# Five Strassen pairs a round in place of three, and row tiles that reach y by an accumulating DMA

## The chip, the cores and the metric

The kernel runs on one core of one Trainium2 chip. The metric is the device time of one execution in microseconds (us), as a median of runs. One more execution is recorded by the hardware profiler; its rows are quoted below.

## The reference

One encoder layer on 256 tokens of width 2048, in float32: a gated feed-forward block (FFN), a mixing block (attention beside a Fourier branch), and a second FFN. The change touches the two FFNs alone. Each computes

```python
def _swiglu(x, w_gate, w_up, w_down):
    return (jax.nn.silu(x @ w_gate) * (x @ w_up)) @ w_down

def _macaron_ffn(x, pre_g, w_gate, w_up, w_down, post_g):
    return x + MACARON_WEIGHT * _rms_norm(_swiglu(_rms_norm(x, pre_g), w_gate, w_up, w_down), post_g)
```

with x of [256, 2048], w_gate and w_up of [2048, 5632] and w_down of [5632, 2048].

## The kernel before, in words

**Products.** Every float32 operand is split in two parts of a shorter type, hi (ScalarE writes it by a copy, line 102) and lo (VectorE subtracts hi from the operand, line 103). One product of a 128x128 activation tile with a 128x512 weight tile is three matmuls on TensorE (`mm3`, lines 107 to 109): hi by hi, hi by lo, lo by hi.

**Weights.** They stream from HBM in pieces of 128x1024 (512 KB, two tiles). `raw_piece` loads a piece by a DMA on SyncE's queue into one of five raw buffers (RAW_BUFS), and `ring` splits it into one of six ring buffers (RING), each with a hi and a lo. A raw buffer comes free when its last reader on ScalarE or VectorE is done, a ring buffer when TensorE's last matmul on it is done.

**Rounds.** An FFN has 11 blocks of 512 hidden columns. Blocks 0 and 1 go through `col_block`. For blocks 2 to 10 the loop at the end of `ffn` runs rounds: `row_line` multiplies the block before the last by its rows of w_down (4 column blocks `cb`, 8 pieces, 12 matmuls each) and adds the result to y, an SBUF buffer; then `swiglu` computes gate and up of the round's own block, with K = 2048 as 16 tiles. A tenth `row_line` follows. That makes nine rounds in each FFN, 18 in all. In the middle of a row_line, ahead of its last column block, `ahead` transposes the h of the block before (8 small matmuls on TensorE, two splits).

**Strassen.** Two K tiles (a pair) times two token tiles by gate and up is a 2x2 by 2x2 block product, eight products if plain. For the pairs in BY_SEVEN `seven` takes Strassen-Winograd's seven: VectorE forms sums of weight tiles (`minus`, line 538: three into a buffer t13, one in place in a raw buffer), four splits follow (three of 128x1024, one of 128x512). In the text F, S, T and Q are these four pieces in their order (6, 6, 6 and 3 matmuls) with the number of their pair; g and u are the two pieces of a plain pair (12 matmuls each), r1 to r8 those of a row_line. Before, BY_SEVEN names groups of four K tiles: the first pair of groups 0, 1 and 2 is done by seven. The activation side is prepared once for each FFN by `Forms.chunk`, four K tiles a call, all four calls during the `col_block`s of block 1.

**Order.** The loop stands under a manual schedule: VectorE, ScalarE and TensorE run their instructions in the order of the program. `Line.feed` makes the preparation of a piece (`ready`: loads, minus, splits) run six pieces ahead of the matmuls (`use`); the work behind a piece's matmuls (`then`: adds, silu, copies into y) stands after `use`, ahead of the next `ready`.

**Into y.** `row_line.out` copies the first round's tiles to y on ScalarE (line 621); in all later rounds VectorE adds them, from PSUM, into y (line 623), eight tiles of 128x512 a round.

Of the kernel before, what the change touches and what calls it, by code (L numbers as in the profile page):

```python
# [18 lines left out]
P = 128  # L19
# [37 lines left out]
def encoder_layer(  # L57
# [371 lines left out]
    class Forms:  # L429
# [3 lines left out]
        def __init__(self, u, rs):  # L433
            self.u, self.rs, self.seven, self.plain = u, rs, {}, {}
            self.rooms = {}

        def room(self, n):

            for i, used in self.rooms.items():
                if used[0] + n <= D:  # L440
                    break
            else:
                i = len(self.rooms)
                used = self.rooms[i] = [0] + [big(f"f{c}{i}", F32R) for c in "hl"]
            used[0] += n
            return [a[:, used[0] - n:used[0]] for a in used[1:]]

# [10 lines left out]
        def chunk(self, kg):  # L458
            ks = slice(kg * CK, (kg + 1) * CK)
            a = chunk.tile([P, CK, S], F32, tag="ch_hi", name="un")  # L460
            for t in range(NT):
                V.tensor_tensor(out=a[:, :, t * P:(t + 1) * P], in0=self.u[t][0][:, ks, :].bitcast(F32),
                                in1=self.u[t][1][:, ks, :].bitcast(F32), op=ALU.add)
            V.tensor_tensor(out=a[:], in0=a[:], in1=self.r[:].unsqueeze(1).to_broadcast([P, CK, S]), op=ALU.mult)
            n = 0
            if kg in BY_SEVEN:
                n = 2
                f = chunk.tile([P, 7, P], F32, tag="ch_lo", name="sf")
                a11, a12, a21, a22 = a[:, 0, 0:P], a[:, 1, 0:P], a[:, 0, P:S], a[:, 1, P:S]
                A.activation(f[:, 0:2, :], a[:, 0:2, 0:P], AF.Copy)  # L470
                A.activation(f[:, 2, :], a22, AF.Copy, scale=-1.0)
                V.tensor_tensor(out=f[:, 3, :], in0=a21, in1=a22, op=ALU.add)
                V.tensor_tensor(out=f[:, 4, :], in0=f[:, 3, :], in1=a11, op=ALU.subtract)
                V.tensor_tensor(out=f[:, 5, :], in0=a11, in1=a21, op=ALU.subtract)
                V.tensor_tensor(out=f[:, 6, :], in0=a12, in1=f[:, 4, :], op=ALU.subtract)
                hi, lo = (x.rearrange("p (a b) -> p a b", b=P) for x in self.room(7 * P))
                split(hi, lo, f[:])
                self.seven[kg] = [(hi[:, i, :], lo[:, i, :]) for i in range(7)]
            hi, lo = (x.rearrange("p (a b) -> p a b", b=S) for x in self.room((CK - n) * S))
            split(hi, lo, a[:, n:, :])  # L480
            for k in range(n, CK):
                self.plain[kg * CK + k] = [(hi[:, k - n, t * P:(t + 1) * P], lo[:, k - n, t * P:(t + 1) * P]) for t in range(NT)]

# [34 lines left out]
    def swiglu(line, forms, w, hs):  # L518
# [38 lines left out]

        def seven(kg, end):
            a11, a12, na22, s1, s2, s3, s4 = forms.seven[kg]
            h = {}  # L560

            def first():
                ra, rb = raw_piece(w[kg], 0), raw_piece(w[kg], 1)
                t = chunk.tile([P, WP, NB], F32, tag=("ch_hi", "ch_lo")[kg % 2], name="t13")
                h.update(ra=ra, rb=rb, t=t)
# [11 lines left out]
            def two(n, a, m, b, last):  # L577
                def use(ws):
# [50 lines left out]
    def ffn(u, rs, wg, wu, wgu, wd, yname, tail, gate0, w_next=None, early=()):  # L629
# [30 lines left out]
        with tc.manual_schedule(engines={mybir.EngineType.DVE, mybir.EngineType.Activation, mybir.EngineType.PE}):  # L660
            for f in range(PLAIN, nblk + 1):
# [568 lines left out]
def _pairs(g, u):  # L1230


    cut = lambda w: w[:, PLAIN * NB:].reshape(KD // CK, CK, P, -1, NB).transpose(3, 0, 2, 1, 4)
    g, u = cut(g), cut(u)
    seven = [g[..., 0, :], u[..., 0, :], u[..., 1, :], g[..., 1, :], g[..., 2, :], g[..., 3, :], u[..., 2, :], u[..., 3, :]]
    plain = [g[..., 0, :], g[..., 1, :], u[..., 0, :], u[..., 1, :], g[..., 2, :], g[..., 3, :], u[..., 2, :], u[..., 3, :]]
    out = np.stack(plain, 3)
    for kg in BY_SEVEN:
        out[:, kg] = np.stack([a[:, kg] for a in seven], 2)
    return np.ascontiguousarray(out).reshape(*out.shape[:3], 2 * CW)  # L1240

# [47 lines left out]
```

## Time and profile before

| | |
|---|---|
| median of 3 runs | 2040.54 us (2039.6 to 2041.2) |
| profiled execution, own time | 2041.46 us |
| its span on the engines | 2039.7 us |
| TensorE busy | 2018.3 us, 99% |
| VectorE busy | 1651.9 us, 81% |
| ScalarE busy | 1112.2 us, 55% |
| GpSimd busy | 50.9 us, 2% |
| granted TensorE clock | 0.999 of full speed |

The span is what the profiler saw from first to last instruction; the time of the execution is 1.8 us longer. PE is TensorE's matmul side and PEld its weight loads, DVE is VectorE, ACT is ScalarE, POOL is GpSimd, SP is SyncE (SPq and POOLq: their queues).

### The profile page before, as it was taken

What the parts mean: (1) busy time and instruction counts of PE and PEld (TensorE: products, weight loads), DVE (VectorE), ACT (ScalarE), POOL (GpSimd) and SP (SyncE); (2) the same over time, 40 slices, a digit from 0 to 9 for tenths busy, and PEclk for the clock granted to TensorE, in tenths of its full rate; (3) what the DMA queues carried; (4) which work ended last, traced back from release to release, by engine and by line L of the source; (5) the groups of instructions that cost most, each with busy time, mean ns of one, the idle gap of its engine ahead of it and who ended that gap; (6) DMA issues with size and microseconds to landing.
All of it is one profiled execution on the core that took longest, in us unless ns stands there. A gap on an engine that the chain in (4) does not pass through costs nothing.

```text
span 2039.7 us, 25718 instructions
## 1 busy us (share of the span) xinstructions
PE 2018.3 (99%) x9308; PEld 1673.0 (82%) x9308; DVE 1651.9 (81%) x2216; ACT 1112.2 (55%) x1490; POOL 50.9 (2%) x46
## 2 busy tenths in 40 slices
PE   9999999999999999999999999999999999999998
PEld 7888888888888878888888888788888888888886
DVE  6878888888888788887877895877788888888876
ACT  7554555544555556556666554555554555544553
POOL 0000000000000110100000000200000000000002
PEclk9999999999999999999999999999999999999999
DMA  8675566556666696964555557566665566656663
GB/s 315 212 271 178 190 218 205 193 175 201 209 207 190 208 294 194 271 187 138 192 190 188 183 179 276 186 207 225 220 203 173 192 218 204 196 174 198 211 209 106
DMA packets 118736, 417.43 MB, mean 205 GB/s; under 512 B 12968, under 2 KB 19120, under 8 KB 116432
## 3 DMA queue, kind: packets, MB, share of 16 engines
q1 hardware_dynamic: 114256, 411.66, 61.1%
q0 software_dynamic: 4352, 4.13, 1.4%
q8 instruction: 73, 1.20, 0.2%
q14 instruction: 55, 0.45, 0.1%
HBM read 409.44 MB, written 6.29 MB: 204 GB/s over the span
## 4 chain that ended last, share of the span: by engine, by line
PE 93%; DVE 4%; DMA 1%; ACT 1%; issue 0%; SPq 0%; DVEq 0%; ACTq 0%
PE pc L108 19%; PE pc L109 19%; PE pc L107 19%; PE pr L109 10%; PE pr L107 10%; PE pr L108 10%; PE pt L177 1%; DVE wlo L103 1%; DMA raw<-in_w_fo 1%; DVE h L390 0%; PE pe L107 0%; PE pe L109 0%; PE pe L108 0%; PE pt L976 0%; PE pf L109 0%
## 5 line engine op out<-in xcount | busy, mean ns | idle before, releaser
L102 ACT ACTIVATE whi<-raw 128x1024 fp32r<-128x1024 f32 (+1 forms) x711 | 749.0, 1059 | 618.8 <-PE pc L109 268.2
L103 DVE TENSOR_TENSOR wlo<-raw,whi 128x1024 fp32r<-128x1024 f32 (+1 forms) x711 | 860.5, 1220 | 277.1 <-ACT whi L102 271.4
L107 PE MATMUL pc<-whi,fh 128*128 128x512 f32 x1098 | 427.1, 389 | 0.0
L108 PE MATMUL pc<-wlo,fh 128*128 128x512 f32 x1098 | 427.1, 389 | 0.0
L109 PE MATMUL pc<-whi,fl 128*128 128x512 f32 x1098 | 427.1, 389 | 0.0
L107 PE MATMUL pc<-whi,uh 128*128 128x512 f32 x688 | 271.7, 395 | 0.2 <-ACT uh L698 0.2
L108 PE MATMUL pc<-wlo,uh 128*128 128x512 f32 x688 | 269.4, 392 | 2.3 <-DVE wlo L103 2.2
L109 PE MATMUL pc<-whi,ul 128*128 128x512 f32 x688 | 269.4, 392 | 1.5 <-DVE ul L103 1.5
L107 PE MATMUL pr<-whi,hTh 128*128 128x512 f32 x688 | 269.4, 392 | 0.0
L109 PE MATMUL pr<-whi,hTl 128*128 128x512 f32 x688 | 267.8, 389 | 0.0
L108 PE MATMUL pr<-wlo,hTh 128*128 128x512 f32 x688 | 267.7, 389 | 0.0
L107 PEld LDWEIGHTS pc<-whi,fh 128*128 128x128 f32 x1098 | 206.1, 188 | 42.8
L109 PEld LDWEIGHTS pc<-whi,fl 128*128 128x128 f32 x1098 | 206.1, 188 | 42.8
L108 PEld LDWEIGHTS pc<-wlo,fh 128*128 128x128 f32 x1098 | 206.1, 188 | 42.7
L109 PEld LDWEIGHTS pc<-whi,ul 128*128 128x128 f32 x688 | 129.4, 188 | 29.2 <-DVE ul L103 2.4
L108 PEld LDWEIGHTS pc<-wlo,uh 128*128 128x128 f32 x688 | 129.5, 188 | 28.9 <-DVE wlo L103 4.0
L107 PEld LDWEIGHTS pc<-whi,uh 128*128 128x128 f32 x688 | 129.5, 188 | 27.0 <-ACT uh L698 1.5
L109 PEld LDWEIGHTS pr<-whi,hTl 128*128 128x128 f32 x688 | 129.1, 188 | 26.9
L108 PEld LDWEIGHTS pr<-wlo,hTh 128*128 128x128 f32 x688 | 129.2, 188 | 26.1
L107 PEld LDWEIGHTS pr<-whi,hTh 128*128 128x128 f32 x688 | 129.2, 188 | 26.1
L102 ACT ACTIVATE whi<-t 128x1024 fp32r<-128x1024 f32 x108 | 90.9, 842 | 98.9 <-DVE t L538 44.5
L103 DVE TENSOR_TENSOR wlo<-t,whi 128x1024 fp32r<-128x1024 f32 x108 | 103.1, 954 | 15.6 <-ACT whi L102 15.6
(333 smaller groups left out, 2066.3 us busy)
## 6 DMA issues: line engine op xcount, KB each, us to landing
raw<-in_f_gu SPq DMA_DIRECT2D x288, 512.0 KB, 4.1
raw<-in_f_down SPq DMA_DIRECT2D x176, 512.0 KB, 5.0
raw<-in_w_in SPq DMA_DIRECT2D x112, 512.0 KB, 4.9
raw<-in_f_up SPq DMA_DIRECT2D x32, 512.0 KB, 4.7
raw<-in_w_ao SPq DMA_DIRECT2D x32, 512.0 KB, 4.0
raw<-in_w_out SPq DMA_DIRECT2D x32, 512.0 KB, 4.0
raw<-in_f_gate SPq DMA_DIRECT2D x31, 512.0 KB, 5.6
fraw<-in_w_f SPq DMA_DIRECT2D x16, 512.0 KB, 5.9
```

Source lines behind the costliest of these rows:

```text
L102: a = A.activation(hi, src, AF.Copy)
L103: v = V.tensor_tensor(out=lo, in0=src, in1=hi.bitcast(F32), op=ALU.subtract)
L107: T.matmul(ps, lh, rh, start=first, stop=False)
L108: T.matmul(ps, lh, rl, start=False, stop=False)
L109: return T.matmul(ps, ll, rh, start=False, stop=last)
L177: T.transpose(pt[:, j, :], src[:, j * P:(j + 1) * P], ident[:])
```

## The change

BY_SEVEN now numbers pairs, and holds five of the eight: pairs 0, 1, 2, 4 and 6. Pairs 0 and 1 follow each other directly; pair 6 closes the seven, with its sums behind its own last pieces. In the row_lines of an FFN but the first and the last (eight of ten) a finished tile is copied by ScalarE from PSUM into a work buffer `part`, and a DMA on GpSimd's queue adds it to y; the first still sets y, and the last still adds on VectorE. The last of the four `forms.chunk` calls moves from the `col_block` into the first row_line of the FFN. The forms are packed without regard to room borders (`put`), so that a split may be cut in two. The host packs the weights to match.

```diff
-BY_SEVEN = (0, 1, 2)
+BY_SEVEN = (0, 1, 2, 4, 6)
+Y_BY_DMA = True
...
-            n = 0
-            if kg in BY_SEVEN:
...
+            for q in range(CK // 2):
+                pair = kg * CK // 2 + q
+                if pair in BY_SEVEN:
...
+                    self.seven[pair] = self.put(f[:])
+                else:
+                    four = self.put(a[:, 2 * q:2 * q + 2, :].rearrange("p k (t c) -> p (k t) c", t=NT))
...
             line.feed(first, two("u0", s4, "g0", a12, False))
             line.feed(second, two("p5", s1, "p7", s3, end))
-            plain(kg, 2, "g", (2, 3))
-            line.feed(lambda: ring(h["ra"][:]), two("p1", a11, "p6", s2, end), *([copy, lambda: add("x2", "p6", "x1")] if end else []))
-            line.feed(lambda: ring(h["t"][:, 0:1, :]), lambda ws: mul("g1", na22, ws[0]),
-                      *([lambda: add("x3", "p7", "x2")] if end else []))
-            plain(kg, 3, "u", (2, 3), *([lambda: add("x2", "p5", "x2")] if end else []))
-
+            if between:
+                between()
+            line.feed(lambda: ring(h["ra"][:]), two("p1", a11, "p6", s2, end), *then[0:2])
+            line.feed(lambda: ring(h["t"][:, 0:1, :]), lambda ws: mul("g1", na22, ws[0]), *then[2:])
...
         for kg in range(KD // CK):
-            if kg in BY_SEVEN:
-                seven(kg, kg == BY_SEVEN[-1])
-                continue
...
+            a, b = 2 * kg, 2 * kg + 1
+            if kg == KD // CK - 1:
+                seven(a, None, *sums)
+                plain(b, 0, *gates)
+                plain(b, 1, *ups)
+            elif b in BY_SEVEN:
+                seven(a)
+                seven(b)
+            else:
+                seven(a, lambda: plain(b, 0))
+                plain(b, 1)
...
-                if first:
+                if way == "set":
                     A.activation(dst, ps[t][:], AF.Copy)
+                elif way == "dma":
+                    part = work("part")
+                    A.activation(part[:], ps[t][:], AF.Copy)
+                    nc.gpsimd.dma_start(dst, part[:], accum_op=ALU.add)
                 else:
                     V.tensor_tensor(out=dst, in0=ps[t][:], in1=dst, op=ALU.add)
...
-                pu = col_block(u, wu, f, between=[lambda: forms.chunk(2), lambda: forms.chunk(3)])
+                pu = col_block(u, wu, f, between=[lambda: forms.chunk(2)])
...
+                way = "set" if f == PLAIN else "dma" if Y_BY_DMA and f < nblk else "add"
+                before = {D // NB - 1: ahead}
+                if f == PLAIN:
+                    before[0] = lambda: forms.chunk(KD // CK - 1)
+                row_line(line, chs[-1] if f > PLAIN else chs[0], wd, f - 2, y, way, before)
```

How the instructions move is shown at three places. The first is VectorE in a row_line of the first FFN, where it prepares the first pair of the coming swiglu (t is the buffer of weight sums, y_927 and y_928 the two halves of y). Before:

```order
L103 TENSOR_TENSOR wlo<-raw,whi 128x1024 x2
L623 TENSOR_TENSOR y_927<-pr,y_927 128x512
L623 TENSOR_TENSOR y_928<-pr,y_928 128x512
L103 TENSOR_TENSOR wlo<-raw,whi 128x1024
L538 TENSOR_TENSOR t_3109<-raw 128x512 x2
L103 TENSOR_TENSOR wlo<-raw,whi 128x1024
L538 TENSOR_TENSOR raw<-raw,t_3109 128x512
L623 TENSOR_TENSOR y_927<-pr,y_927 128x512
L623 TENSOR_TENSOR y_928<-pr,y_928 128x512
L103 TENSOR_TENSOR wlo<-t_3109,whi 128x1024
```

Now:

```order
L545 TENSOR_TENSOR t_2704<-raw 128x512 x2
L104 TENSOR_TENSOR wlo<-raw,whi 128x1024
L545 TENSOR_TENSOR raw<-raw,t_2704 128x512
L104 TENSOR_TENSOR wlo<-t_2704,whi 128x1024
L545 TENSOR_TENSOR t_2704<-raw 128x512
L104 TENSOR_TENSOR wlo<-raw,whi 128x1024
L104 TENSOR_TENSOR wlo<-t_2704,whi 128x512
L104 TENSOR_TENSOR hTl<-pt,hTh 128x4x128 x2
L545 TENSOR_TENSOR t_2809<-raw 128x512 x2
L104 TENSOR_TENSOR wlo<-raw,whi 128x1024
```

The additions into y are gone from VectorE's order, and the pieces of pair 1 (S and T with no plain piece between them) follow those of pair 0.

The second place is ScalarE in the same stretch, from the silu of one round to the transposed h (hTh). Before:

```order
L551 ACTIVATE x_4499<-x_4499 128x512
L102 ACTIVATE whi<-raw 128x1024 x5
L102 ACTIVATE whi<-t_4666 128x1024
L102 ACTIVATE whi<-raw 128x1024 x2
L102 ACTIVATE hTh<-pt 128x4x128 x2
```

Now:

```order
L558 ACTIVATE x_3697<-x_3697 128x512
L103 ACTIVATE whi<-raw 128x1024 x3
L637 ACTIVATE part<-pr 128x512 x2
L103 ACTIVATE whi<-raw 128x1024 x2
L637 ACTIVATE part<-pr 128x512 x2
L103 ACTIVATE whi<-t_3814 128x1024
L103 ACTIVATE whi<-raw 128x1024
L637 ACTIVATE part<-pr 128x512 x2
L103 ACTIVATE whi<-t_3814 128x512
L103 ACTIVATE hTh<-pt 128x4x128 x2
L103 ACTIVATE whi<-raw 128x1024
L637 ACTIVATE part<-pr 128x512 x2
```

Eight copies a round stand between the splits, two behind each column block.

The third is SyncE's queue in the first round of the first FFN, where the loads for the FFN's end (h, gpost and gpre, 1 MB each) stand among the weight pieces. Before:

```order
L83 DMA raw<-in_f_gu 128x1024 x4
L83 DMA h_1891<-in_x 128x2048
L83 DMA raw<-in_f_gu 128x1024
L83 DMA h_1893<-in_x 128x2048
L83 DMA raw<-in_f_gu 128x1024 x2
L83 DMA gpost_1895<-in_f_post 128x2048
L83 DMA raw<-in_f_gu 128x1024
L83 DMA gpre_1897<-in_mix_pre 128x2048
```

Now:

```order
L84 DMA raw<-in_f_gu 128x1024 x3
L84 DMA h_1979<-in_x 128x2048
L84 DMA raw<-in_f_gu 128x1024 x2
L84 DMA h_1981<-in_x 128x2048
L84 DMA raw<-in_f_gu 128x1024 x2
L84 DMA gpost_1983<-in_f_post 128x2048
L84 DMA gpre_1985<-in_mix_pre 128x2048
L84 DMA raw<-in_f_gu 128x1024 x9
```

gpost and gpre now stand next to each other, ahead of the eighth weight piece of the round.

## Rows read from the trace of the kernel before

**Rows 1.** The page, busy time of each engine: us, share of the span, instructions.

```profile
PE 2018.3 (99%) x9308; PEld 1673.0 (82%) x9308; DVE 1651.9 (81%) x2216; ACT 1112.2 (55%) x1490; POOL 50.9 (2%) x46
```

**Rows 2.** The page, the chain that ended last, shares of the span by engine.

```profile
PE 93%; DVE 4%; DMA 1%; ACT 1%; issue 0%; SPq 0%; DVEq 0%; ACTq 0%
```

**Rows 3.** Timeline of PE, rounds 4 and 5: start us, us, engine, line, what.

```profile
304.41 1.03 PE L177 MATMUL pt<-ident,x 128*128 128x128 f32 x8
305.20 0.48 PE L107 MATMUL pr<-whi,hTh 128*128 128x512 f32 x1
...
310.74 0.39 PE L107 MATMUL pc<-whi,fh 128*128 128x512 f32 x1
...
344.74 0.39 PE L107 MATMUL pc<-whi,fh 128*128 128x512 f32 x1
...
374.87 0.39 PE L107 MATMUL pc<-whi,fh 128*128 128x512 f32 x1
```

**Rows 4.** Busy time by stretch: one round; the stretch with GpSimd's accumulating loads.

```profile
core 0: us, PE busy (x) PEld busy (x) DVE busy (x) ACT busy (x) POOL busy (x), PEclk, DMA share, GB/s
310.74:374.80 64.06, 64.06 (x288) 53.17 (x287) 53.35 (x62) 32.71 (x35) 0.00 (x0) 1.00 0.61 197
716.00:866.00 150.00, 144.86 (x721) 120.20 (x720) 126.05 (x228) 86.98 (x157) 20.03 (x19) 1.00 0.84 253
```

**Rows 5.** Groups of instructions by shape: count, busy us, mean ns, idle before and releasers.

```profile
L103 DVE TENSOR_TENSOR wlo<-raw,whi 128x1024 fp32r<-128x1024 f32 x709 | 859.1, 1222 | 273.8 <-ACT whi L102 268.1
L102 ACT ACTIVATE whi<-raw 128x1024 fp32r<-128x1024 f32 x709 | 747.8, 1060 | 617.2 <-PE pc L109 268.2 <-PE pr L109 237.7 <-issue 76.1
L538 DVE TENSOR_TENSOR t<-raw 128x512 f32<-128x512 f32 x162 | 106.9, 688 | 1.8
L103 DVE TENSOR_TENSOR wlo<-t,whi 128x512 fp32r<-128x512 f32 x54 | 37.2, 688 | 13.0 <-ACT whi L102 13.0
L102 ACT ACTIVATE whi<-t 128x512 fp32r<-128x512 f32 x54 | 33.6, 622 | 27.8 <-issue 27.8
L623 DVE TENSOR_TENSOR yf<-pr,yf 128x512 f32<-128x512 f32 x72 | 47.0, 686 | 5.3 <-PE pr L109 5.3
L621 ACT ACTIVATE yf<-pr 128x512 f32<-128x512 f32 x8 | 4.8, 598 | 4.6 <-PE pr L109 4.6
```

**Rows 6.** Timeline of DVE, one Strassen pair of round 4 with its neighbours.

```profile
313.22 1.29 DVE L538 TENSOR_TENSOR t<-raw 128x512 f32<-128x512 f32 x2
...
318.02 2.36 DVE L103 TENSOR_TENSOR wlo<-raw,whi 128x1024 fp32r<-128x1024 f32 x2
320.29 0.69 DVE L103 TENSOR_TENSOR wlo<-t,whi 128x512 fp32r<-128x512 f32 x1
322.28 1.23 DVE L103 TENSOR_TENSOR wlo<-raw,whi 128x1024 fp32r<-128x1024 f32 x1 [1.30 <-ACT whi L102]
```

**Rows 7.** Timeline of ACT, a split that waits for its ring buffer.

```profile
312.34 1.07 ACT L102 ACTIVATE whi<-raw 128x1024 fp32r<-128x1024 f32 x1 [0.30 <-PE pc L109]
```

**Rows 8.** DMAs into raw from 374.8 to 438.85 (one round).

```profile
L83 SPq DMA_DIRECT2D raw<-in_f_gu x16: 327/328/328, 377.5 to 435.3; - x16
L83 SPq DMA_DIRECT2D raw<-in_f_down x8: 327/328/328, 397.9 to 410.7; - x8
...
DMA to landing us min/median/max: 3.5/4.8/5.7
```

**Rows 9.** DMA queues: one round (310.74 to 374.8): packets, MB, share of 16 engines.

```profile
q1 hardware_dynamic: 3459, 12.59, 60.5%
```

**Rows 10.** The same from 716 to 866, where GpSimd issues accumulating loads.

```profile
q0 software_dynamic: 4080, 3.87, 17.8%
```

**Rows 11.** Line 827, GpSimd's accumulating loads into fraw (252 KB each): durations, landing.

```profile
L827 POOL DMA_DIRECT2D fraw<-in_w_f x16: 1072/1088/1225, 717.5 to 865.4; - x16
...
DMA to landing us min/median/max: 4.5/7.0/10.2
```

**Rows 12.** DMAs into raw from 716 to 866.

```profile
DMA to landing us min/median/max: 3.7/5.1/9.4
```

**Rows 13.** Timeline of DVE, small sums of `forms.chunk`.

```profile
61.52 0.29 DVE L472 TENSOR_TENSOR sf<-un 128x128 f32<-128x128 f32 x1
61.72 0.29 DVE L474 TENSOR_TENSOR sf<-un 128x128 f32<-128x128 f32 x1
```

More of the change, by code (lines that the diff above doesn't have):

```diff
@@ L434, in __init__, with put @@
             self.u, self.rs, self.seven, self.plain = u, rs, {}, {}
[L435 to L446, printed above, removed]
+            self.rooms, self.used = [], KD
+        def put(self, src):
+            out, n = [], src.shape[1]
+            while len(out) < n:
+                if self.used == KD:
+                    self.rooms, self.used = [big("f" + c, F32R, [P, KD, P]) for c in "hl"], 0
+                a = len(out)
+                m = min(n - a, KD - self.used)
+                hi, lo = (r[:, self.used:self.used + m, :] for r in self.rooms)
+                split(hi, lo, src[:, a:a + m, :])
+                out += [(hi[:, i, :], lo[:, i, :]) for i in range(m)]
+                self.used += m
+            return out
         def rows(self):
@@ L464, in chunk @@
             V.tensor_tensor(out=a[:], in0=a[:], in1=self.r[:].unsqueeze(1).to_broadcast([P, CK, S]), op=ALU.mult)
-            n = 0
-            if kg in BY_SEVEN:
[L467 to L482, printed above, removed]
+            for q in range(CK // 2):
+                pair = kg * CK // 2 + q
+                if pair in BY_SEVEN:
+                    f = chunk.tile([P, 7, P], F32, tag="ch_lo", name="sf")
+                    k0, k1 = 2 * q, 2 * q + 1
+                    a11, a12, a21, a22 = a[:, k0, 0:P], a[:, k1, 0:P], a[:, k0, P:S], a[:, k1, P:S]
+                    A.activation(f[:, 0:2, :], a[:, k0:k1 + 1, 0:P], AF.Copy)
+                    A.activation(f[:, 2, :], a22, AF.Copy, scale=-1.0)
+                    V.tensor_tensor(out=f[:, 3, :], in0=a21, in1=a22, op=ALU.add)
+                    V.tensor_tensor(out=f[:, 4, :], in0=f[:, 3, :], in1=a11, op=ALU.subtract)
+                    V.tensor_tensor(out=f[:, 5, :], in0=a11, in1=a21, op=ALU.subtract)
+                    V.tensor_tensor(out=f[:, 6, :], in0=a12, in1=f[:, 4, :], op=ALU.subtract)
+                    self.seven[pair] = self.put(f[:])
+                else:
+                    four = self.put(a[:, 2 * q:2 * q + 2, :].rearrange("p k (t c) -> p (k t) c", t=NT))
+                    for i in range(2):
+                        self.plain[2 * pair + i] = four[NT * i:NT * i + NT]
@@ L527, in mul, with raw, plain @@
             begun.add(n)
-        def plain(kg, i, c, ks, *then):
+        def raw(pair, i):
+            return raw_piece(w[pair // 2], pair % 2 * 2 + i)
+        def plain(pair, i, *then):
             def use(b):
                 for t in range(NT):
-                    for j, k in enumerate(ks):
-                        mul(c + str(t), forms.plain[kg * CK + k][t], b[j], kg * CK + k == KD - 1)
-            line.feed(lambda: ring(raw_piece(w[kg], i)[:]), use, *then)
+                    for j in range(2):
+                        k = 2 * pair + j
+                        mul("gu"[i] + str(t), forms.plain[k][t], b[j], k == KD - 1)
+            line.feed(lambda: ring(raw(pair, i)[:]), use, *then)
         def minus(out, a, b):
@@ L556, in times, with seven @@
             hs.append(up)
-        def seven(kg, end):
-            a11, a12, na22, s1, s2, s3, s4 = forms.seven[kg]
+        def seven(pair, between=None, *then):
+            a11, a12, na22, s1, s2, s3, s4 = forms.seven[pair]
+            end = pair == BY_SEVEN[-1]
             h = {}
             def first():
-                ra, rb = raw_piece(w[kg], 0), raw_piece(w[kg], 1)
-                t = chunk.tile([P, WP, NB], F32, tag=("ch_hi", "ch_lo")[kg % 2], name="t13")
+                ra, rb = raw(pair, 0), raw(pair, 1)
+                t = chunk.tile([P, WP, NB], F32, tag=("ch_hi", "ch_lo")[BY_SEVEN.index(pair) % 2], name="t13")
                 h.update(ra=ra, rb=rb, t=t)
@@ L608, in use @@
                 if i == 0:
-                    if cb == D // NB - 1:
-                        ahead()
+                    if cb in ahead:
+                        ahead[cb]()
                     ps.extend(pmm.tile([P, NB], F32, tag="mm", name="pr") for _ in range(NT))
@@ L1230, in _pairs @@
 def _pairs(g, u):
-    cut = lambda w: w[:, PLAIN * NB:].reshape(KD // CK, CK, P, -1, NB).transpose(3, 0, 2, 1, 4)
+    cut = lambda w: w[:, PLAIN * NB:].reshape(KD // 2, 2, P, -1, NB).transpose(3, 0, 1, 2, 4)
     g, u = cut(g), cut(u)
[L1235 to L1240, printed above, removed]
+    out = np.stack([g[:, :, 0], g[:, :, 1], u[:, :, 0], u[:, :, 1]], 3)
+    for q in BY_SEVEN:
+        out[:, q] = np.stack([g[:, q, 0], u[:, q, 0], u[:, q, 1], g[:, q, 1]], 2)
+    out = out.reshape(-1, KD // CK, 2, P, 4 * NB).transpose(0, 1, 3, 2, 4)
+    return np.ascontiguousarray(out).reshape(-1, KD // CK, P, 2 * CW)
 def _rows(w):
```

13 lines of the change are left out of this document (5 added, 8 removed).

## The prediction, made before the changed kernel ran

> **What bounds the kernel now.** I read the page's busy times and the chain first. TensorE is busy for 2018.3 of 2039.7 us [rows 1], and 93% of the chain that ended last lies on it [rows 2]: time can only be won by fewer matmuls, or lost by TensorE waiting. The timeline gives the price of a matmul: 150 start from 310.74 to 344.74, one each 0.2267 us [rows 3] (the 0.39 us of a row is pipelined). A round takes 374.87 - 310.74 = 64.13 us [rows 3]; its 96 matmuls of rows and 183 of products make 63.2, the eight transposes 0.8 (304.41 to 305.20). So TensorE never waits in a round. VectorE is busy 53.35 us of it, ScalarE 32.71 [rows 4].
>
> Why VectorE's idle time costs nothing: the split that finds its ring buffer taken waits for TensorE. ScalarE's split at 312.34 starts 0.24 us after matmul six of the round (310.74 + 6 x 0.2267 = 312.10) has freed the buffer [rows 3, 7], and the groups name TensorE as the releaser of 506 of 617 us of idle ahead of the splits [rows 5]. Preparation runs the full six pieces ahead; the kernel has a reserve there, and the change spends it.
>
> **TensorE's gain.** Seven products for eight in two more pairs: 2 x 3 = 6 matmuls a round, 108 in 18 rounds, 108 x 0.2267 = 24.5 us. The profiled execution would go from 2041.46 to 2017.0, and the median, 0.9 below it, from 2040.54 to 2016.0. A round becomes 62.77 us.
>
> **VectorE's load.** A plain pair costs it two splits of 1.222, a seven-pair four differences of 0.688, three splits of 1.222 and one of 0.688 [rows 5]: 7.11 against 2.44, so 9.3 us more a round. The eight additions into y, 0.686 each [rows 5], are 5.5 less. 53.35 + 9.3 - 5.5 = 57.2 of 62.8 us, 91%: it fits on average. ScalarE gets 2 x (1.06 + 0.62) = 3.4 of splits and 8 x 0.60 = 4.8 of copies [rows 5]: 40.9, no bound. The average hides the question, whether preparation stays ahead through the seven-pairs of one swiglu.
>
> **The ledger of a round.** Back to back, two splits take 2.36, so a further one 1.14; two differences 1.29, so a further one 0.60 [rows 6]. A seven-pair of before takes VectorE from 313.22 to 320.98 with one plain piece inside, 6.6 us without it [rows 6]; TensorE needs 21 x 0.2267 = 4.76. A plain pair is 2.3 against 5.44, a piece of rows 1.14 against 2.72. Let TensorE start F0 at 0; then it wants F2 at 9.5, S2 at 10.9, g3 at 12.2, F4 at 19.7, S4 at 21.1, g5 at 22.4. In the 17 us ahead of that VectorE has 12.7 us of work (F0 to S1, two splits of h), so it is ahead as far as the ring lets it. S1's ring buffer comes free at 0 (the end of r8). There ScalarE has its two copies of r8 ahead of the split (0.24 + 2 x 0.53), then the split (1.06) and VectorE's (1.14): S1 is ready at 3.6, not at 2.5. From there VectorE runs without a pause: T1 5.4, Q1 6.0, F2 8.3, S2 10.2, g3 12.0. The reserve is down to 0.2 us at g3. With the additions still on VectorE (eight, some 5 us of the 17 ahead) it would not be ahead at 0 at all, and would lose 1 to 2 us there.
>
> The raw buffers next. b, the second piece of pair 4, takes the buffer that pair 2's b frees, at the end of S2's last difference, 10.8. Landing takes 3.5 to 5.7 us [rows 8], so it is there at 14.3 to 16.5; VectorE comes to it at 15.5: a wait of 0 to 1.0. F4 is ready at 17.3 to 18.3 (wanted 19.7), S4 at 19.2 to 20.2 (21.1), g5 at 20.9 to 21.9 (22.4). Pair 6 repeats this. So a round hides everything if landings stay near 4.8, and has 0.2 to 0.5 us to spare in two places. Ten handovers at 0.05 more each than I counted, or a landing at the top end, cost some tenths. I take 0.3 us a round for the 16 rounds that are not first, 5 us; bounds 0 and, if each of the two reserves misses by 0.5, 16.
>
> **The DMA that adds.** No row shows one of 128 packets of 2 KB within SBUF. The nearest are the accumulating loads into fraw: 1.09 us on GpSimd, 7.0 us to landing [rows 11]. In their stretch software packets take 17.8% of 16 engines for 150 us, 427 us for 4080 packets, 0.105 us each at 0.95 KB [rows 10]; weight packets take 0.179 at 3.64 KB [rows 9]. A line through both puts 2 KB at 0.135 us; 144 packets (16 more than rows, as the fraw loads have: 272 for 256) on 16 engines make 1.2 us of all engines for one add. Bounds: 0.95 if a packet costs the same at any size, 1.8 by bytes. Eight are 7.6 to 14.4 us beside the round's 0.605 x 64.06 = 38.8 [rows 9], up to 53 of 62.8. Who waits for an add: the copy of r8's tiles takes the buffer of r2's, some 17 us later, against 10.2 + 1.2 at worst [rows 11]; the next round's add, 60 us later. So none is late; only the weight loads beside them are slower.
>
> **First rounds.** `forms.chunk` moves there: VectorE pays 2 x 0.60 + 1.14 for the products, 4 x 0.2 for small sums [rows 13] and 1.6 for two splits, 4.7 us, under TensorE's 22 us of rows where VectorE has 3 to spare; the col_block gives up about as much, where VectorE had kept up. On SyncE gpost and gpre now stand together ahead of u3's piece: 2 MB, at 38.8/24 = 1.6 us per 512 KB 6.4 us. u3's buffer frees at 5.4, the piece lands at 15.3 to 17.5, and has to be there at 14.6. That is 0.7 to 2.9 late, and what the two loads of h leave behind comes on top. I take 5 us for the first FFN (0 to 11) and, with one load fewer, 1 for the second (0 to 6).
>
> **Sum.** 2016.0 + 5 + 5 + 1 = **2027 us**.
>
> **Rivals.**
> *A: the reserve is missed.* Each step of the ledger is a little longer, or loads land at 6 us and more beside the adds; weight loads beside accumulating ones have a median of 5.1 and a maximum of 9.4 [rows 12], against 4.8 and 5.7 [rows 8]. TensorE then waits at g3, g5 and T6, 0.9 to 1.5 us a round: 2016 + 6 + 16 x (0.9 to 1.5) = 2036 to 2046. Against it: the adds fall into the rows, where VectorE has 4 us to spare, and are through when the seven-pairs draw their later loads.
> *B, slower: the adds fill the queues.* From r1 to r8, 22.5 us, eight weight loads take 12.9. With eight adds at 1.2 that is exactly full; at 1.8 it is 27.3, and the loads for pairs 0 and 1 come 4.8 us later. The raw and ring buffers and VectorE's spare 4 us swallow that much. From about 2.1 us an add on, the 62.77 us round loses the excess: 8 x 0.3 = 2.4 us a round or more, against a break-even of (24.5 - 6)/16 = 1.2. At 2.2 us: 2016 + 6 + 16 x 3 = 2070. For it: no row has SBUF as the source; against it, the bound by bytes is 1.8.
> *C: GpSimd cannot issue.* If GpSimd could write an add's packets only while VectorE stands still, 8 x 1.09 = 8.7 us a round would have 5.6 of VectorE's idle, and copies, then splits, would wait 3 us a round: 2016 + 6 + 48 = 2070. The rows speak against it: the 16 issues took 1.07 to 1.23 us [rows 11] in a stretch where VectorE was busy for 126 of 150 us [rows 4]. The Trainium skill has such a rule (SBUF — State Buffer, section "SBUF: two separate sides", the "DVE blocks DMA" trap: GpSimd's descriptor writes are locked out while VectorE holds the port pair that they share). By that rule it would happen with VectorE's operations in their two-port modes; the trace shows no sign of it for these shapes.
> *D: the change does not do what it says.* The matmul count is certain from the order (six fewer a round); that the additions leave VectorE too. What remains is a wait of 1.4 us a round or more that eats the gain exactly: that is A's upper end.
>
> **Chances.** Forecast (2016 to 2035) 0.67, A 0.18, B 0.11, C 0.04. Around 2040.5, 0.2% is 4.1 us, about what a measurement tells from no change (three runs lie within 1.6). A lies a fifth below 2036.4, most between, a fifth above 2044.6. Faster 0.67 + 0.04 = 0.71, same 0.11, slower 0.03 + 0.11 + 0.04 = 0.18. The range 2017 to 2046 leaves out B and C (0.15) and little below: some products without any wait; the likeliest case's own range is 2017 to 2035.
>
> **What would show it.** TensorE 108 matmuls fewer, a steady round between 62.8 and 63.3 us, VectorE busy for 57 of it, ScalarE for 41. TensorE's idle, if any, at g3, g5 or T6 behind VectorE's wlo, and in the first rounds at u3 behind the load. Adds landing within 10 us, GpSimd at 1.1 us an issue, raw loads near 5 us. The prediction is wrong if steady rounds take over 63.7 us; if then wlo waits for whi and whi for raw, it is the loads (A or B, told apart by the add's packet time); if GpSimd's issues are long, C; if TensorE waits for VectorE without any load late, the ledger.

## The result, and the profile after

The changed kernel takes **2016.95 us** (median of four runs, 2016.12 to 2018.05), beside 2040.24 us (2039.6 to 2041.2) for the kernel before: ratio 0.9886, 95% interval 0.9869 to 0.9903. That is 23.3 us faster. The forecast was 2027 us; its range, 2017 to 2046, began just above the measured time.

The page of the kernel after: busy time of each engine, then the chain by engine.

```profile
PE 1993.5 (99%) x9200; PEld 1652.1 (82%) x9200; DVE 1728.4 (86%) x2324; ACT 1231.5 (61%) x1702; POOL 160.9 (8%) x174
...
PE 93%; DVE 4%; DMA 1%; ACT 1%; issue 1%; SPq 0%; DVEq 0%; ACTq 0%
```

Against [rows 1 and 2], TensorE has 108 matmuls and 24.8 us less, and is as much on the chain as before. VectorE went up by 76 us, ScalarE by 119, GpSimd by 110 (128 adds), and the shares of VectorE and ScalarE on the chain are unchanged.

The timeline of PE, F0's first matmul in two rounds that follow each other (pc are the PSUM buffers of the gate and up products, pr those of a row_line; where a row ends in brackets, they hold the idle time before it and what ended it):

```profile
306.52 0.39 PE L108 MATMUL pc<-whi,fh 128*128 128x512 f32 x1
...
369.30 0.39 PE L108 MATMUL pc<-whi,fh 128*128 128x512 f32 x1
```

A round takes 369.30 - 306.52 = 62.78 us, the 62.77 that were worked out from 64.13 in [rows 3]. The busy times of that round (columns as in [rows 4]):

```profile
306.52:369.30 62.78, 62.78 (x283) 52.07 (x281) 56.81 (x67) 39.67 (x47) 6.90 (x9) 1.00 0.78 234
```

TensorE waits for nothing in it; VectorE has 6.0 us left, where it had 10.7. All eight rounds of the first FFN between first matmuls, from 118.21 to 620.39, last 62.77 or 62.78 us; the first is no exception. In the second FFN seven of the eight do, and one takes 62.93.

The timeline of DVE from S1 to g3, the piece that the ledger called the tightest, then its row for g5, and what ScalarE did ahead of S1. The last two rows of ScalarE are the splits of S1 and T1:

```profile
308.35 1.23 DVE L104 TENSOR_TENSOR wlo<-t,whi 128x1024 fp32r<-128x1024 f32 x1 [1.38 <-ACT whi L103]
...
310.22 1.22 DVE L104 TENSOR_TENSOR wlo<-raw,whi 128x1024 fp32r<-128x1024 f32 x1
311.36 0.69 DVE L104 TENSOR_TENSOR wlo<-t,whi 128x512 fp32r<-128x512 f32 x1
...
313.18 1.22 DVE L104 TENSOR_TENSOR wlo<-raw,whi 128x1024 fp32r<-128x1024 f32 x1
...
314.92 1.22 DVE L104 TENSOR_TENSOR wlo<-t,whi 128x1024 fp32r<-128x1024 f32 x1
...
316.78 2.36 DVE L104 TENSOR_TENSOR wlo<-raw,whi 128x1024 fp32r<-128x1024 f32 x2
...
325.59 2.35 DVE L104 TENSOR_TENSOR wlo<-raw,whi 128x1024 fp32r<-128x1024 f32 x2
```

```profile
305.41 0.60 ACT L637 ACTIVATE part<-pr 128x512 f32<-128x512 f32 x1 [0.30 <-PE pr L110]
306.77 0.60 ACT L637 ACTIVATE part<-pr 128x512 f32<-128x512 f32 x1 [0.76 <-PE pr L110]
307.27 1.05 ACT L103 ACTIVATE whi<-t 128x1024 fp32r<-128x1024 f32 x1
308.22 1.05 ACT L103 ACTIVATE whi<-raw 128x1024 fp32r<-128x1024 f32 x1
```

Set these against the ledger, with F0 at 306.52. S1 is ready at 309.58, that is 3.1 after F0 (ledger 3.6); then VectorE runs without a pause (the rows left out are weight differences), as the ledger has it: T1 4.9 (5.4), Q1 5.5 (6.0), F2 7.9 (8.3), S2 9.6 (10.2), g3, the first of the two splits at 316.78, 11.4 (12.0). g3 is wanted at 12.2. Some 0.8 us are left there, not 0.2. The 0.5 us come from one place: the ledger put both copies of r8's tiles behind F0, but the first tile is finished six matmuls before the second, so its copy (305.41) was over by then, and only one stood ahead of S1's split. The ledger's second tight place, g5, had more room than it said: 20.3 after F0 (20.9 to 21.9), wanted at 22.4, so 2.1 us are left where 0.5 to 1.5 were expected.

The landings, of the adds, and of the raw pieces of the round from 306.5 to 369.3:

```profile
L638 POOL DMA_DIRECT2D y<-part x64: 847/856/1001, 163.7 to 621.7; - x64
L638 POOL DMA_DIRECT2D yf<-part x64: 847/856/1186, 1462.9 to 1920.9; - x64
...
DMA to landing us min/median/max: 3.3/6.3/9.2
```

```profile
DMA to landing us min/median/max: 3.7/5.2/7.4
```

An add takes GpSimd 0.86 us (1.09 in [rows 11]) and lands within 9.2. The raw loads are a little slower than in [rows 8], with a median of 5.2 against 4.8 and a maximum of 7.4 against 5.7. The queues of the same round:

```profile
q1 hardware_dynamic: 3452, 12.58, 58.2%
q0 software_dynamic: 1119, 2.04, 19.6%
```

19.6% of 16 engines for 62.8 us over 1119 packets is 0.176 us a packet, 1.58 us of all engines for an add of 144 packets: the estimate was 1.2, its bounds 0.95 and 1.8.

### The profile page after: what moved, and what is told of

Same layout as the page of the kernel before. It is cut to its first block, busy times and chain, and to the rows that moved or that the text cites. A ratio compares the mean times of both kernels' runs of the same rounds, so it can differ in the third digit from the quotient of the medians.

```text
span 2014.4 us, 26315 instructions
## 1 busy us (share of the span) xinstructions
PE 1993.5 (99%) x9200; PEld 1652.1 (82%) x9200; DVE 1728.4 (86%) x2324; ACT 1231.5 (61%) x1702; POOL 160.9 (8%) x174
## 4 chain that ended last, share of the span: by engine, by line
PE 93%; DVE 4%; DMA 1%; ACT 1%; issue 1%; SPq 0%; DVEq 0%; ACTq 0%
PE pc L108 19%; PE pc L109 19%; PE pc L110 19%; PE pr L108 10%; PE pr L110 10%; PE pr L109 10%; PE pt L178 1%; DVE wlo L104 1%; DMA raw<-in_w_fo 1%; DVE h L391 1%; PE pe L108 0%; PE pe L109 0%; PE pe L110 0%; PE pt L997 0%; PE pf L110 0%
## 5 line engine op out<-in xcount | busy, mean ns | idle before, releaser
L103 ACT ACTIVATE whi<-raw 128x1024 fp32r<-128x1024 f32 (+1 forms) x711 | 741.2, 1055 | 392.9 <-PE pc L110 117.4
L108 PE MATMUL pc<-whi,fh 128*128 128x512 f32 x1062 | 413.1, 389 | 0.0
L109 PE MATMUL pc<-wlo,fh 128*128 128x512 f32 x1062 | 413.1, 389 | 0.0
L110 PE MATMUL pc<-whi,fl 128*128 128x512 f32 x1062 | 413.1, 389 | 0.0
L110 PEld LDWEIGHTS pc<-whi,fl 128*128 128x128 f32 x1062 | 199.3, 188 | 41.5
L108 PEld LDWEIGHTS pc<-whi,fh 128*128 128x128 f32 x1062 | 199.3, 188 | 41.5
L109 PEld LDWEIGHTS pc<-wlo,fh 128*128 128x128 f32 x1062 | 199.3, 188 | 41.3
L104 DVE TENSOR_TENSOR wlo<-t,whi 128x1024 fp32r<-128x1024 f32 (+1 forms) x180 | 171.5, 953 | 48.0 <-ACT whi L103 48.0
L103 ACT ACTIVATE whi<-t 128x1024 fp32r<-128x1024 f32 (+1 forms) x180 | 152.1, 845 | 93.2 <-DVE t L545 92.9
L545 DVE TENSOR_TENSOR t<-raw 128x512 f32<-128x512 f32 x270 | 178.0, 687 | 3.1
```

The costliest lines, as they stand in the source:

```text
L103: a = A.activation(hi, src, AF.Copy)
L104: v = V.tensor_tensor(out=lo, in0=src, in1=hi.bitcast(F32), op=ALU.subtract)
L108: T.matmul(ps, lh, rh, start=first, stop=False)
L109: T.matmul(ps, lh, rl, start=False, stop=False)
L110: return T.matmul(ps, ll, rh, start=False, stop=last)
L545: V.tensor_tensor(out=out, in0=a, in1=b, op=ALU.subtract)
```

## The experiments

Each was timed in turn with the kernel before on the same chip; the medians of the kernel before were 2040.2 to 2040.5 us. Differences from the changed kernel are taken from its 2016.95 us above.

### e1_adds_on_vector: five sevens alone

```diff
-Y_BY_DMA = True
+Y_BY_DMA = False
```

> Five sevens, but all tiles reach y by VectorE's additions as before; the DMA adds and ScalarE's copies are gone. Theory (the ledger's reserve of 0.8 us ahead of g3 is all there is, and the DMA adds made it): VectorE gets 5.5 us more a round, 62.3 of 62.8 us, and TensorE waits 1 to 2 us in each of 16 rounds: 2033 to 2049 us. Rival (the seven-pairs alone make the gain, the additions fit into VectorE's idle time): 2015 to 2020 us.

Measured: **2029.39 us**, ratio 0.9945 (0.9928 to 0.9961): 12.4 us more than with the adds. The round from 307.12 on in its windows, and PE's timeline at the wait:

```profile
307.12:370.57 63.45, 63.23 (x282) 51.93 (x281) 61.33 (x75) 35.40 (x39) 0.00 (x0) 1.00 0.59 199
```

```profile
319.48 0.39 PE L108 MATMUL pc<-whi,fh 128*128 128x512 f32 x1
320.09 0.50 PE L109 MATMUL pc<-wlo,fh 128*128 128x512 f32 x1 [0.22 <-DVE wlo L104]
```

319.48 is 12.4 after F0: g3, the place of the ledger. Its second matmul, the first that needs lo, starts 0.61 us after the first instead of 0.23. The eight rounds between first matmuls lose 4.4 us in the first FFN and 6.7 in the second, 0.7 a round, where 1 to 2 were expected; the time lies between the ranges of theory and rival. So seven products alone win 11 us, and the adds on the DMA win as much again.

### e2_three_by_dma: the DMA adds alone

```diff
...
-                if first:
+                if way == "set":
                     A.activation(dst, ps[t][:], AF.Copy)
+                elif way == "dma":
+                    part = work("part")
+                    A.activation(part[:], ps[t][:], AF.Copy)
+                    nc.gpsimd.dma_start(dst, part[:], accum_op=ALU.add)
...
```

> The kernel before, with three sevens, and only the way into y changed: ScalarE copies and the DMA adds. Theory (TensorE never waited in a round, so VectorE's 5.5 us less are worth nothing and the adds disturb nobody): 2038 to 2043 us, VectorE busy for about 48 us of a 64.1 us round. Rival (the adds slow the weight loads enough for TensorE to wait): 2046 us or more. Second rival (VectorE did hold TensorE up somewhere): 2036 us or less.

Measured: **2040.76 us**, ratio 0.9999 (0.9990 to 1.0009). VectorE is busy for 1575.8 us against 1651.9 in [rows 1], and that is worth nothing. Together with e1 that says: these 76 us, 4.8 in each of the 16 row_lines, pay only where the seven-pairs have used up VectorE's lead.

### e3_four_sevens: half the step

```diff
-BY_SEVEN = (0, 1, 2, 4, 6)
+BY_SEVEN = (0, 2, 4, 6)
```

> Pairs 0, 2, 4 and 6 by seven, pair 1 plain; everything else as changed. Theory (time follows the count of matmuls, 0.2267 us each, no round waits): 54 matmuls more than with five, 12.2 us: 2029 us, between 2027 and 2031. Rival (five sevens already lose something in each round that shows in no wait): less than 12 us apart, 2020 to 2026 us.

Measured: **2029.53 us**, ratio 0.9946 (0.9931 to 0.9961), 12.6 us above five sevens and 10.9 below the kernel before; 54 matmuls are 12.2. The time follows the count of matmuls in both steps.

### e4_chunk_back: the moved call moved back

```diff
-                pu = col_block(u, wu, f, between=[lambda: forms.chunk(2)])
+                pu = col_block(u, wu, f, between=[lambda: forms.chunk(2), lambda: forms.chunk(3)])
...
-                if f == PLAIN:
-                    before[0] = lambda: forms.chunk(KD // CK - 1)
```

> The changed kernel with the last forms.chunk call back in the col_block of block 1 in both FFNs. By the prediction's step (the move costs up to 5 us in the first FFN and 1 in the second): 2011 us. Theory after the trace (gpost and gpre left the queue 9 us ahead of u3's load, so nobody waited): 2015 to 2019 us. Rival (the move was needed, since the col_block has no room on VectorE for a second call): 2020 us or more, with TensorE waiting at the start of the rounds.

Measured: **2016.68 us**, ratio 0.9883 (0.9868 to 0.9898), the changed kernel's time. The move of the call costs nothing and brings nothing. It says nothing of the two 1 MB loads, because they stay together ahead of u3's piece when the call moves back. The timeline of SPq in e4:

```profile
112.15 0.43 SPq L84 DMA_DIRECT2D gpost<-in_f_post  x1
112.67 0.38 SPq L84 DMA_DIRECT2D gpre<-in_mix_pre  x1
```

No run has them apart; what they cost is read from the changed kernel's first round, which takes 62.77 us like the others. Why the loads between the weight pieces did no harm stands in the changed kernel's timeline of SPq in the first round, where F0 is at 118.21:

```profile
112.13 1.43 SPq L84 DMA_DIRECT2D raw<-in_f_gu  x2
113.61 0.42 SPq L84 DMA_DIRECT2D gpost<-in_f_post  x1
114.09 0.42 SPq L84 DMA_DIRECT2D gpre<-in_mix_pre  x1
122.01 1.42 SPq L84 DMA_DIRECT2D raw<-in_f_gu  x2
```

The queue came to gpost and gpre at 113.6, eight us before the buffer for u3 came free (122.01, that is 3.8 after F0; the prediction had 5.4). They moved their 2 MB while SyncE waited for that buffer: issue to landing is 8.2 and 10.2 us, so they were through at 121.8 and 124.3. ScalarE split u3's piece without a wait for it, 10.9 after F0 (its timeline); the prediction had it land at 15.3 to 17.5.

```profile
129.13 1.05 ACT L103 ACTIVATE whi<-raw 128x1024 fp32r<-128x1024 f32 x1
```

### e5_one_more_difference and e6_three_more_differences: how much reserve

One, or three, further copies of the first difference of pair 2 (e5's edit; e6 has `range(3)`):

```diff
                 minus(t[:, 0, :], ra[:, 1, :], ra[:, 0, :])
+                if pair == 2:
+                    for _ in range(1):
+                        minus(t[:, 0, :], ra[:, 1, :], ra[:, 0, :])
```

> The changed kernel with the first weight difference of pair 2 formed twice in each round: 0.60 us more for VectorE ahead of F2, S2 and g3. Theory (the trace of the changed kernel has 0.8 us left ahead of g3, the least in a round): nothing is lost, 2015 to 2019 us. Rival (the prediction's ledger, 0.2 us left there): 0.4 us in each of 16 to 18 rounds, 2023 to 2025 us.

> The same difference formed four times, 1.80 us more for VectorE at that place. Theory (0.8 us left): TensorE waits 1.0 us at g3 in each of 16 to 18 rounds, 2033 to 2036 us. The prediction's ledger: 1.6 us a round, 2042 to 2047 us. Rival (VectorE has 6 us idle in a round, which take it up): 2015 to 2019 us.

Measured: **2019.81 us** (2017.55 to 2023.30), ratio 0.9899 (0.9882 to 0.9916), and **2045.99 us**, ratio 1.0023 (1.0013 to 1.0032). The differences of e6 in DVE's timeline, and PE behind them (F0 at 310.71):

```profile
316.16 3.46 DVE L545 TENSOR_TENSOR t<-raw 128x512 f32<-128x512 f32 x5
```

```profile
320.23 0.39 PE L108 MATMUL pc<-whi,fh 128*128 128x512 f32 x1
320.81 0.50 PE L109 MATMUL pc<-wlo,fh 128*128 128x512 f32 x1 [0.20 <-DVE wlo L104]
...
322.08 0.39 PE L108 MATMUL pc<-whi,fh 128*128 128x512 f32 x1
322.55 0.50 PE L109 MATMUL pc<-wlo,fh 128*128 128x512 f32 x1
...
323.82 0.39 PE L108 MATMUL pc<-whi,fh 128*128 128x512 f32 x1
324.41 0.50 PE L109 MATMUL pc<-wlo,fh 128*128 128x512 f32 x1 [0.21 <-DVE wlo L104]
```

TensorE waits at F2, S2 and g3, and a round takes 64.15 us, 1.4 more. Five differences took 3.46 us where two take 1.29: one more that repeats the one before costs 0.72, not the 0.60 of the expectation. 3 x 0.72 - 0.8 = 1.4: the reserve of 0.8 us holds. Over 18 rounds 1.4 us make 25, so 2042 us, which is what the profiled run took (2042.5); the median of the ten runs lies 3.5 us higher, and this profile does not show why. In e5 0.72 us fit in, and no round waits at g3, though its median is 0.8 us above the theory's range (the runs lie 5.8 apart). In its profile the rounds lose 1.0 us in the first FFN (three rounds of 63.03 to 63.18 us) and 2.4 in the second (up to 63.66), all at another place (the waits of PE in the second FFN; us in total, times, longest):

```profile
PE pr L108 <- DVE x L550: 1.1, 3, 0.6
```

There the second row tile of r1 waits for a PSUM buffer that one of VectorE's additions out of PSUM (line 550) frees. That second tight place was not in the ledger; e8 shows it large.

### e7_adds_doubled: rival B

```diff
                     nc.gpsimd.dma_start(dst, part[:], accum_op=ALU.add)
+                    nc.gpsimd.dma_start(out_dram[t * P:(t + 1) * P, cb * NB:(cb + 1) * NB], part[:], accum_op=ALU.add)
```

`out_dram` is the kernel's output in HBM, so the second add is not quite the first one over again: its target lies in HBM and not in SBUF.

> Every tile that a DMA adds to y is added by a second DMA to rows of the output in HBM, which are written over at the end: twice the packets of the adds. The changed kernel's queues in one round: weights 36.5 us of all 16 engines, adds 12.3 us. Theory (a packet's time is its engine's own): 61.1 of 62.8 us, of which 37.5 fall on the 22.6 us of rows, so the weight loads of pairs 1 to 4 come up to 15 us late and TensorE waits 2 us a round or more: 2050 us and up. Rival (much of a packet's time is waiting that overlaps): 2015 to 2025 us.

Measured: **2054.95 us**, ratio 1.0068 (1.0053 to 1.0083): 38 us more than the changed kernel. Its queues in the round from 312.00 to 376.88, and PE's timeline:

```profile
q1 hardware_dynamic: 3473, 12.65, 55.0%
q0 software_dynamic: 2332, 4.24, 37.9%
```

```profile
335.30 0.50 PE L110 MATMUL pc<-wlo,fh 128*128 128x512 f32 x1 [0.20 <-DVE wlo L105]
...
355.42 0.50 PE L109 MATMUL pr<-whi,hTh 128*128 128x512 f32 x1 [1.02 <-DVE x L551]
```

A packet still takes 0.17 us, so a tile now costs 3.0 us of all engines and the queues are 93% busy. The gate and up loads land after 8.7 us in the median (5.2 in the changed kernel), ScalarE waits for them (5.3 us ahead of the split at 329.33, F4's), and the round takes 64.88 us: 2.1 more. Rival B's mechanism exists; one add, at 1.58 us, stays below the 2.1 us from which the prediction had it cost time. What the excess costs was overestimated there: 0.9 us above it cost 2.1 a round, not 8 x 0.9.

### e8_six_sevens and e12_six_spread: one pair more

```diff
-BY_SEVEN = (0, 1, 2, 4, 6)
+BY_SEVEN = (0, 1, 2, 4, 5, 6)
```

and in e12 `(0, 2, 3, 4, 5, 6)`.

> Pairs 0, 1, 2, 4, 5 and 6 by seven: three matmuls fewer a round, 12.2 us in all, 2004.7 us if nothing waits. VectorE gets 4.67 us more, 61.5 of a 62.1 us round. Theory (the reserve is spent, so VectorE, with its waits for ScalarE, sets the round, at 62.5 to 63.5 us): no gain over five, 2012 to 2030 us. Rival (the six pieces of lead carry it): 2004 to 2008 us.

> Six sevens on pairs 0, 2, 3, 4, 5 and 6, the plain pair again behind the first; tiles reach y by the DMA adds. If the place of the plain pair alone had made e8's waits: 2005 to 2012 us. Theory (five seven-pairs in a row spend 5 x 1.8 us, more than any lead of six pieces; VectorE then ends the swiglu late and the row tile waits for its PSUM buffer, as in e8): 2060 to 2110 us.

Measured: **2104.16 us**, ratio 1.0307 (1.0289 to 1.0325), and **2128.18 us**, ratio 1.0424 (1.0408 to 1.0440). Both lie above the ranges of their theories, which ended at 2030 and 2110 us. In e8 a round takes 65.7 to 68.8 us, where its matmuls need 62.1. The waits of PE over the whole of e8 (us in total, times, longest), its timeline in one round (F0 at 323.52), and two stretches behind that wait:

```profile
PE pr L108 <- DVE x L550: 44.2, 18, 3.4
PE pc L109 <- DVE wlo L104: 9.2, 38, 1.0
```

```profile
365.49 0.39 PE L110 MATMUL pr<-whi,hTl 128*128 128x512 f32 x1
368.55 0.50 PE L108 MATMUL pr<-whi,hTh 128*128 128x512 f32 x1 [2.68 <-DVE x L550]
```

```profile
369.90:373.20 3.30, 3.30 (x9) 2.55 (x8) 2.43 (x3) 2.87 (x4) 0.00 (x0) 0.50 0.30 110
373.40:376.00 2.60, 2.60 (x13) 2.13 (x13) 2.56 (x4) 1.67 (x3) 1.34 (x2) 1.00 0.70 210
```

Most is not lost at a weight piece. At the end of the swiglu VectorE is late with its additions out of PSUM, and the second row tile of r1 waits for a PSUM buffer that one of them frees: 2.5 us in each of 18 rounds. Behind that wait the granted clock is 0.50, the lower of its two levels (1.2 GHz), for 3.3 us, in which matmuls start 0.43 us apart and not 0.23. That is so in 12 of the 16 rounds between first matmuls (67.4 to 68.8 us); in the other four the clock stays at 1.00 behind the wait (65.7 to 66.1 us). In the changed kernel the same addition ends at 347.2 and the row tile wants the buffer at 348.0: 0.8 us of reserve there too. e12 shows that another place for the plain pair is no help: TensorE's waits for the additions are 47.9 us there, and those for wlo grow to 23.9.

### e11_spread_adds_on_vector: is it the order or the load?

```diff
-BY_SEVEN = (0, 1, 2, 4, 6)
-Y_BY_DMA = True
+BY_SEVEN = (0, 2, 3, 4, 6)
+Y_BY_DMA = False
```

> Five sevens on other pairs, 0, 2, 3, 4 and 6, so that a plain pair stands between the first seven-pair and the next; the additions on VectorE, as in e1. The lead is counted in pieces (six), and a seven-pair's pieces carry 6, 6, 6 and 3 matmuls where a plain pair's carry 12 each: ahead of the third pair in the order the lead is 8.8 us of TensorE instead of 5.4. Theory (e1 lost its 0.65 us a round at g3 because three seven-pairs in a row follow the rows): no wait at g3, 2015 to 2021 us although VectorE is as full as in e1. Rival (VectorE at 62.3 of 62.8 us is simply too full): 2027 us or more.

Measured: **2032.14 us**, ratio 0.9955 (0.9939 to 0.9972). PE's timeline of one round:

```profile
350.13 0.39 PE L110 MATMUL pr<-whi,hTl 128*128 128x512 f32 x1
351.18 0.50 PE L108 MATMUL pr<-whi,hTh 128*128 128x512 f32 x1 [0.66 <-DVE x L550]
```

The theory fell in its time and stood in its place: nothing waits at g3 any more, but VectorE is just as full (busy for 245.4 of 256 us from 310 to 566, in e1 for 246.0), and the wait turns up at the row tile's PSUM buffer (11.0 us in 16 waits), with rounds of 63.2 to 64.3 us. The better order only moved the wait: the engine behind it had no time left.

### e9_six_gpsimd_one and e10_seven_gpsimd_two: work for GpSimd

In e9, with the six pairs of e8 (e10 takes the first difference and a seventh pair as well):

```diff
...
-            V.tensor_tensor(out=up[:], in0=up[:], in1=g[:], op=ALU.mult)
+            nc.gpsimd.tensor_tensor(out=up[:], in0=up[:], in1=g[:], op=ALU.mult)
...
                 minus(ra[:, 1, :], rb[:, 0, :], t[:, 0, :])
+                nc.gpsimd.tensor_tensor(out=rb[:, 0, :], in0=ra[:, 1, :], in1=rb[:, 1, :], op=ALU.subtract)
...
-                minus(h["t"][:, 0, :], h["ra"][:, 1, :], h["rb"][:, 1, :])
...
-            line.feed(lambda: ring(h["t"][:, 0:1, :]), lambda ws: mul("g1", na22, ws[0]), *then[2:])
+            line.feed(lambda: ring(h["rb"][:, 0:1, :]), lambda ws: mul("g1", na22, ws[0]), *then[2:])
```

> The six sevens of e8, with work taken from VectorE: GpSimd forms the fourth weight difference of each pair (from the raw buffers, into the first half of the second one) and the two products of silu and up. VectorE loses 6 x 0.60 + 2 x 0.65 = 4.9 us a round, 56.6 of 61.4 us. Theory (e8 lost its time because VectorE's work between F0 and the end of the swiglu was too much, at F2, S2 and at the row tile's PSUM buffer): 2005 to 2012 us. Rival (the lead is spent by the seven-pairs themselves, or GpSimd's operations of 1.43 us come late or slow VectorE): 2020 us and up.

> Seven sevens (all pairs but the last), and GpSimd forms the first and the fourth weight difference of each pair and the products of silu and up: 16 operations of 1.43 us and eight adds of 0.86 us, 30 us a round. TensorE 24.5 us less than with five, 1992.5 us if nothing waits; VectorE 56.4 of 60.7 us. Theory (VectorE's load is all that stood in the way): 1993 to 2005 us. Rival (GpSimd's first difference comes late for S, or its operations slow VectorE's): 2015 us and up.

Measured: **2143.25 us**, ratio 1.0503 (1.0453 to 1.0552), and **2267.56 us**, ratio 1.1107 (1.1088 to 1.1125). The theory fell. (The rounds of the expectations are 0.7 us too short: TensorE needs 62.1 in e9 and 61.4 in e10. Both are missed by far more.) GpSimd's groups in e9 (count, busy us, mean ns), DVE's timeline beside one of these differences (GpSimd's ran from 205.22 to 207.37), and VectorE's largest group in e8 and then in e9:

```profile
L578 POOL TENSOR_TENSOR raw<-raw 128x512 f32<-128x512 f32 x108 | 249.8, 2313 | 605.4 <-DVE raw L545 408.7 <-DMA raw<-in_f_gu 103.9 <-ACT whi L103 92.7
...
L372 POOL TENSOR_TENSOR yo<-yo,gpost 128x512 f32<-128x512 f32 x8 | 11.4, 1426 | 439.3 <-ACT junk L371 439.3
```

```profile
205.00 1.22 DVE L104 TENSOR_TENSOR wlo<-t,whi 128x1024 fp32r<-128x1024 f32 x1
206.35 2.71 DVE L104 TENSOR_TENSOR wlo<-raw,whi 128x1024 fp32r<-128x1024 f32 x2
```

```profile
L104 DVE TENSOR_TENSOR wlo<-raw,whi 128x1024 fp32r<-128x1024 f32 x709 | 854.0, 1221 | 146.3 <-ACT whi L103 145.0
L104 DVE TENSOR_TENSOR wlo<-raw,whi 128x1024 fp32r<-128x1024 f32 x709 | 931.1, 1326 | 173.5 <-ACT whi L103 164.6
```

The 108 differences take GpSimd 2.31 us each in the mean; the same shape takes 1.43 on line 372, where VectorE has some work too, and 1.28 at the least there. Two splits of VectorE take 2.71 us beside one of these, 2.36 elsewhere [rows 6]. 144 operations (88 us by the prices of the expectation) were taken from VectorE, and its busy time did not fall: 1803.7 us in e9, 1804.0 in e8. The time came back in its splits: the 709 from raw take 77 us more in e9, and the 108 of 128x1024 from t 15 more (146.9 against 132.0). The Trainium skill (SBUF — State Buffer, section "SBUF: two separate sides") says that a GpSimd operation that reads SBUF and a VectorE operation with two SBUF inputs lock each other out of a shared port pair for a whole instruction. The trace agrees in kind, though VectorE lost 0.6 us for each of GpSimd's operations, not the 1.28 or more of a whole one. What else slows e9 beyond e8 was not taken apart (TensorE's waits for wlo grow from 9.2 to 33.8 us; a raw buffer is held longer in it).

## Why the prediction was right and wrong

**What bounds the kernel, and the gain: right.** 108 matmuls at 0.2267 us are 24.5; measured 23.3 (19.8 to 26.7 by the interval), and e3 splits it in 10.9 and 12.6, where half of the matmuls are 12.2. The steady round came out to 0.01 us.

**VectorE's and ScalarE's load: right.** 56.81 and 39.67 us a round, against 57.2 and 40.9.

**The step that failed is the stall term of the sum, 5 + 5 + 1 = 11 us; it measured about 1** (24.5 - 23.3, less than the interval can tell from 0). The trace has no wait in it: in 15 of the 16 rounds the matmuls take the 62.77 us of their count, and in one 0.16 more. The range failed with it: with its own lower bounds, 0 in all three parts, the sum makes 2016.0 us, and the forecast's chance was given for 2016 to 2035, but the range set aside "some products without any wait" and began at 2017. That case came true. In its parts:

- *Steady rounds, "I take 0.3 us a round": 0.* The ledger's place and course were right, its reserve at g3 too small by 0.6 us, most of it from one copy on ScalarE that was counted behind F0 and lay ahead of it. (The terms for S1 make 3.5, not the 3.6 written there; with one copy they make 3.0, and the trace has 3.1.) e5 and e6 put the reserve at 0.8 from both sides: 0.72 us fit in, and of 2.17 TensorE waits for 1.4. Besides, a reserve that comes out positive predicts no wait; adding 0.3 us for handovers that might be longer turned an uncertainty into a cost.
- *First round, "0.7 to 2.9 late", taken as 5: 0.* The two 1 MB loads were timed from the moment at which u3's buffer frees. They need no raw buffer, so the queue issued them 8 us earlier, in SyncE's own waiting time; and that buffer came free at 3.8, not at 5.4. The moved call's work on VectorE cost nothing either (e4).
- *Second FFN, 1: 0*, for the same reason.

**The additions on VectorE, "1 to 2 us a round": the right place, about half the size** (0.7, e1).

**The DMA add: mis-sized within its bounds,** 1.58 us for 1.2, with nothing behind it. Its packets, most of 2 KB, took 0.176 us, as long as the 3.64 KB weight packets in [rows 9], where a line through two packet sizes gave 0.135.

**The rivals.** A is what e6 makes of the kernel, and it needed 2.2 us more on VectorE. B is what e7 makes of it, with twice the packets. C has nothing for it: 128 issues at 0.86 us, and the split is as fast as before (1.221 us, [rows 5] 1.222). The prediction left out the second reserve, the PSUM buffer that passes from the swiglu's sums to the row tile. It was 0.8 us, so the time did not suffer, but each experiment that loads VectorE or the queues further meets it.

No variant beat the changed kernel (e4's time is the same): with five pairs its rounds take no longer than their matmuls, with six VectorE cannot follow.

## What to carry to other kernels

- Two changes that are worth 11 us and 0 us alone were worth 23 together: relief for an engine off the path pays only once another part of the change has spent its reserve, so cost such parts in each other's company.
- When a ledger says that the work is ready in time, forecast no wait and put the doubt into the range, which then has to reach down to the time without any wait. For each load in a queue, date its issue by what it waits for itself, not by its neighbour.
- Look for every buffer that passes between stages, PSUM too. A lead that is counted in pieces shrinks where the pieces get smaller, and the tightest handover decides, not the average load.

## What the runs showed of the hardware that was not expected

- GpSimd's elementwise operations are no free help beside a busy VectorE (2.31 us for a difference, and the 88 us that VectorE gave away came back in its splits, e9), while its 128 DMA issues left VectorE's splits as fast as before (1.221 us, [rows 5] 1.222).
- An add of 256 KB within SBUF costs as much queue time as a weight piece of 512 KB: 1.58 us of all 16 engines, against 58.2% of 62.8 us for 24 pieces, 1.52 each.
- A wait of 2.7 us of TensorE was followed by 3.3 us at half the granted clock (e8), which made it about half as dear again: eight starts came 0.2 us late each. In four of 16 rounds with such waits the clock did not fall.
- A VectorE operation that repeats the one before it, into the same buffer, took 0.72 us instead of 0.60 (e6). Whether the engine or a wait of the program's own makes the difference is not shown.
